# Two attentions whose value products alternate between output halves, with score tiles of 64 rows and one masked-maximum step

## The chip, the cores and the metric

The kernel runs on one core of a Trainium2 chip. The metric is the device time of one execution in microseconds (us); shorter is better. The engines are PE (matrix products: MATMUL, with its weight loads as a row of their own, PEld), DVE (VectorE), ACT (ScalarE), POOL (GpSimd) and SP, which issues loads. PE writes to PSUM only; a tile named `mm`, `bg` or `ax` lies there, a tile named `b` in SBUF.

## The reference, cut to what matters

Two transformer blocks run over 256 tokens of a stream x and 256 of a context. Most of the work is feed-forward and projection products. The change touches the two softmax attentions over 512 keys. In the first block (the "odd" mixer) there are 16 heads of 64 features; keys and values are shared by four heads each, a window mask covers the keys of x, and a learned `sink` takes part in the softmax:

```python
s_band = where(valid, einsum('bqhgd,bkhd->bhgqk', qj, kj), -inf)   # valid: |q - k| <= 128
s_ctx = einsum('bqhgd,bkhd->bhgqk', qj, kc)
p = softmax(concatenate([sink, s_ctx, s_band], -1), -1)
out = einsum('bhgqk,bkhd->bqhgd', p_ctx, vc) + einsum('bhgqk,bkhd->bqhgd', p_band, vj)
```

In the second block (latent attention, called MLA below) there are 16 heads with 96 features in a score and 64 in a value, without mask and sink:

```python
p = softmax(scale * (q_nope . k_nope + q_rope . k_rope), -1)
out = p @ v
```

## The kernel before, in words

Everything is float32. A product that needs precision in the large projections is made of three products of parts, hi·hi, hi·lo and lo·hi, each part exact in the format fp32r (`split`, L604 and L605, makes the parts: ACT the hi, DVE the lo). Products of plain float32 tiles, such as the values, are issued by the compiler as two MATMULs each.

Both attentions call `attention(units, pre, order)`. A unit is one head and 128 of the 256 queries against all 512 keys; each attention has 32 units, and `order` is "s0 e1 n1 t3 v4 f0": in step i the scores of unit i are emitted, exponential and normalisation of unit i-1, transposes of unit i-3, value products of unit i-4, and then filling work. Per unit:

- `st0`: `scores()` leaves [128 queries, 512 keys] in a PSUM tile of pool `mm` (5 tiles). DVE takes the negated maximum (L1427) and, in the odd mixer, the minimum of it and -sink (L1429).
- `st1`: ACT makes exp(score - max) with the row sum (L1436, followed by a read of the accumulator), and exp(sink - max) (L1439); DVE adds the two (L1440).
- `st2`: DVE takes the reciprocal (L1444) and scales the row (L1445).
- `st3`: PE transposes four 128x128 squares (L1451) into a PSUM tile `ax` (2 tiles), and ACT copies it to SBUF as PT (L1453).
- `st4`: `values(PT)`: four products of V[b], 64 columns wide, with 128 columns of PT each, summed in one half of a PSUM tile: partitions 0 to 63 for s = 0, 64 to 127 for s = 1 (`tile_position=(0, 64*s)`; L1578 in the odd mixer, L2213 in MLA). After eight units `split` takes the tile away.

In the odd mixer a score needs 64 rows only. The keys of two heads lie in one tile, features on partitions; before, `k_split` (L1508) makes for each key head s a pair of tiles in which the other 64 rows are zero, set by POOL. So each unit issues three products of 128 rows by 512 columns (L1567, L1569, L1570) and between them one bf16 product of the identity with the mask, 128 columns (L1568). In MLA a score is three products of 96 rows (L582 to L584).

Units that follow each other are s = 0 and s = 1 of the same head group and queries. The tile framework orders the instructions of each engine when the kernel is built, by what it expects to be ready; each engine then issues in that order. The weights of the projections come by DMA from the queue of SP, and ACT and DVE split them (L574, L575). The other column-tiled product of the kernel is the output of the state-space scan, `y` (L2349), whose inner loop alternates s = 0 and s = 1.

Of the kernel before, what the change touches and what calls it, by code (L numbers as in the profile page):

```python
# [48 lines left out]
F32 = mybir.dt.float32  # L49
# [7 lines left out]
P = 128  # L57
# [11 lines left out]
# ---------------------------------------------------------------- host layout  # L69
# [44 lines left out]
def _pack_tok(w):  # L114
    """Pieces of 4 blocks of rows by 512 columns, the column halves one after the other."""
# [181 lines left out]
# ---------------------------------------------------------------- the program  # L297
# [5 lines left out]
class Beat:  # L303
    """Emission order of work that waits on long chains: after(k, f) emits f once k more blocks of products are out."""
# [23 lines left out]
class Prog:  # L328
# [19 lines left out]
    def in_order(self):  # L348
        """Each compute engine issues what this block emits in the order of its emission."""
# [11 lines left out]
    def behind_now(self):  # L361
        """What this block emits is issued behind what has been emitted."""
# [9 lines left out]
    def behind(self):  # L372
        """What this block emits is issued behind the last block in order."""
# [7 lines left out]
    # ---- tiles  # L381
# [13 lines left out]
    def po(self):  # L395
        """Accumulators of attention outputs, alternating between two pools."""
# [23 lines left out]
    def consts(self):  # L420
# [7 lines left out]
        self.cstb = cp.tile([P, 3 * P], BF16, name="cstb")  # L428
# [20 lines left out]
    # ---- modulation vectors  # L449
# [5 lines left out]
    def mods(self, ci, w, bias, M, i0, cnt, post):  # L455
        """Steps that compute modulation vectors i0 .. i0+cnt-1 of M, one weight slab each."""
# [86 lines left out]
    def tick(self, n=1.0):  # L543
        """Emit background steps worth n."""
# [41 lines left out]
    def pair3(self, ps, W, X, first, last):  # L586
        """Both halves of one block of rows, the products that need the lo part of X behind the others."""
# [19 lines left out]
    # ---- rms statistics of one half (256 tokens), features on partitions  # L607
# [23 lines left out]
    def rstd2(self):  # L631
        """r1 = rms(h)^-1 and r12 = r1 * rms(h * fin * r1)^-1, as columns r12, r12, r1, r1.
# [1869 lines left out]
```

## Time and profile before

| | |
|---|---|
| median of 3 runs | 2310.92 us (2307.32 to 2318.86) |
| profiled execution, its span (the page tells its time by this) | 2305.9 us |
| instructions | 33864 |
| PE busy over the span | 2247.0 us, 97% |
| DVE, ACT, POOL busy over the span | 1564.9, 975.2, 166.7 us |
| odd attention, first score product to last value product | 1448.6 to 1532.5 us of the span |
| MLA attention, the same | about 1980 to 2081 us |

The page names PE first, and the chain of work that ended last is 76% PE. A matmul's end is modelled and overlaps the next one's start, so the cost of a matmul is read from one start to the next, not from its duration. On ACT and DVE too an instruction begins about 0.1 us before the one ahead is put down as ended, so the busy time of a stretch (in which overlaps count once) is less than the sum of the durations.

### The profile page before, as it was taken

Reading aid. Unit: us, or ns where it says so; the run is one execution under the profiler, and the core shown is the slowest. Engines: PE = TensorE matmul, PEld = TensorE weight load, DVE = VectorE, ACT = ScalarE, POOL = GpSimd, SP = SyncE. Lnnn points to the kernel's source line nnn. Section 1 sums busy time; section 2 is a strip of 40 time slices with the busy share of each in tenths; the row PEclk is TensorE's granted clock in tenths of the full one; section 3 lists DMA queues with packets and bytes.
Section 4 is the critical chain, followed back from the end, with each engine's and each line's share of the span. In section 5 each row is a group of like instructions: output and inputs, shape, how many; then the busy total and the mean of one; then the engine's idle time right before and its main releaser. Section 6 shows DMA issues by size and latency. Waiting matters only on the chain.

```text
span 2305.9 us, 33864 instructions
## 1 busy us (share of the span) xinstructions
PE 2247.0 (97%) x13706; PEld 1956.2 (85%) x13706; DVE 1564.9 (68%) x2447; ACT 975.2 (42%) x1651; POOL 166.7 (7%) x185
## 2 busy tenths in 40 slices
PE   7999999999899999999999999999999899999998
PEld 6888888888898888898878889789999788888997
DVE  5887774734897666468748647757556898666664
ACT  4222223544542222243222335656445566665553
POOL 0000000001300000000000002101000553000000
PEclk8999999999999999999999999999999999999999
DMA  7665552221145455325657623114554323213553
GB/s 266 218 232 182 185 204 83 92 101 74 56 160 187 155 192 183 146 92 201 242 173 285 231 92 115 57 56 169 184 183 160 133 88 122 85 60 126 184 175 120
DMA packets 58076, 348.54 MB, mean 151 GB/s; under 512 B 6464, under 2 KB 10048, under 8 KB 22848
## 3 DMA queue, kind: packets, MB, share of 16 engines
q1 hardware_dynamic: 56544, 344.22, 42.1%
q8 instruction: 108, 1.77, 0.3%
q0 software_dynamic: 512, 1.05, 0.2%
q10 hardware_dynamic: 864, 1.11, 0.2%
q14 instruction: 48, 0.39, 0.0%
HBM read 343.73 MB, written 1.05 MB: 150 GB/s over the span
## 4 chain that ended last, share of the span: by engine, by line
PE 76%; issue 13%; DVE 5%; POOL 3%; ACT 1%; DMA 1%; SPq 0%; POOLq 0%; DVEq 0%; ACTq 0%
PE mm L582 21%; PE mm L584 20%; PE mm L583 20%; PE mm L591 6%; PE ax L1451 1%; DVE wl L575 1%; POOL b L1727 1%; PE bg L531 1%; PE bg L1578 1%; PE bg L2213 1%; PE mm L1578 1%; PE mm L2213 1%; DMA b<-mod 1%; POOL b L1728 1%; DVE acc L616 0%
## 5 line engine op out<-in xcount | busy, mean ns | idle before, releaser
L582 PE MATMUL mm<-b,wh 128*128 128x512 f32 (+1 forms) x2764 | 958.5, 348 | 3.6 <-DVE c L1617 1.9
L584 PE MATMUL mm<-b,wl 128*128 128x512 f32 (+1 forms) x2764 | 947.7, 344 | 3.6 <-DVE wl L575 3.5
L583 PE MATMUL mm<-b,wh 128*128 128x512 f32 (+1 forms) x2764 | 949.5, 344 | 0.0
L575 DVE TENSOR_TENSOR wl<-wr,wh 128x1024 fp32r<-128x1024 f32 (+2 forms) x474 | 553.7, 1173 | 392.0 <-ACT wh L574 385.5
L574 ACT CAST wh<-wr 128x1024 fp32r<-128x1024 f32 (+2 forms) x474 | 473.7, 1006 | 575.8 <-PE mm L583 389.8
L582 PEld LDWEIGHTS mm<-b,wh 128*128 128x128 f32 x2764 | 527.0, 191 | 78.3 <-issue 8.5
L584 PEld LDWEIGHTS mm<-b,wl 128*128 128x128 f32 x2764 | 526.1, 191 | 65.7 <-DVE wl L575 5.0
L583 PEld LDWEIGHTS mm<-b,wh 128*128 128x128 f32 x2764 | 527.3, 191 | 61.0 <-issue 1.9
L522 DVE SCALAR_TENSOR_TENSOR ma<-mr,cs,ma 128x1024 f32<-128x1024 f32 x252 | 311.5, 1278 | 32.9 <-DMA mr<-ada 28.8
L591 PE MATMUL mm<-b,wh 128*128 128x256 f32 x1408 | 254.5, 283 | 0.0
L591 PEld LDWEIGHTS mm<-b,wh 128*128 128x128 f32 x1408 | 220.3, 192 | 0.2 <-ACT b L604 0.2
L591 PE MATMUL mm<-b,wl 128*128 128x256 f32 x704 | 184.4, 283 | 0.0
L591 PEld LDWEIGHTS mm<-b,wl 128*128 128x128 f32 x704 | 135.5, 192 | 0.0
L927 ACT ACTIVATE s<-mm 128x512 f32<-128x512 f32 x66 | 39.5, 599 | 222.2 <-PE mm L584 222.1
L582 PE MATMUL mm<-wh,b 128*128 128x512 f32 (+1 forms) x264 | 100.1, 380 | 1.9 <-ACT b L604 1.9
L583 PE MATMUL mm<-wl,b 128*128 128x512 f32 (+1 forms) x264 | 99.5, 377 | 0.0
L584 PE MATMUL mm<-wh,b 128*128 128x512 f32 (+1 forms) x264 | 99.3, 377 | 0.0
L629 POOL TENSOR_TENSOR rr<-rv,nhalf 128x2 f32<-128x2 f32 x15 | 15.6, 1043 | 991.6 <-DVE rv L628 991.6
L604 ACT CAST b<-s 128x512 fp32r<-128x512 f32 x70 | 43.2, 617 | 73.4 <-DVE s L928 64.9
L928 DVE TENSOR_TENSOR s<-s,mm 128x512 f32<-128x512 f32 x66 | 45.2, 684 | 40.3 <-PE mm L584 40.3
L1427 DVE TENSOR_REDUCE mx<-mm 128x1 f32<-128x512 f32 x64 | 43.8, 687 | 31.9 <-PE mm L1570 17.5
L983 DVE SCALAR_TENSOR_TENSOR h<-mm,M,h 128x256 f32<-128x256 f32 x144 | 59.6, 476 | 7.5 <-PE mm L584 7.5
(357 smaller groups left out, 2072.8 us busy)
## 6 DMA issues: line engine op xcount, KB each, us to landing
wr<-win SPq DMA_DIRECT2D x88, 1024.0 KB, 4.8
mr<-ada SPq DMA_DIRECT2D x56, 1024.0 KB, 4.9
wr<-wout SPq DMA_DIRECT2D x40, 768.0 KB, 4.4
mr<-mod SPq DMA_DIRECT2D x26, 1024.0 KB, 5.0
wr<-b_up SPq DMA_DIRECT2D x22, 1024.0 KB, 4.9
wr<-wout SPq DMA_DIRECT2D x14, 1024.0 KB, 4.8
wr<-b_xbc SPq DMA_DIRECT2D x11, 1024.0 KB, 4.9
wr<-b_down SPq DMA_DIRECT2D x10, 1024.0 KB, 4.9
```

Source lines behind the costliest of these rows:

```text
L522: nc.vector.scalar_tensor_tensor(hold["a"][s][:, c], raw[:, c], v, hold["a"][s][:, c], op0=ALU.mult, op1=ALU.add)
L574: nc.scalar.copy(hi, r)
L575: (nc.gpsimd if k0 // kk in pool else nc.vector).tensor_sub(lo, r, hi.bitcast(F32))
L582: nc.tensor.matmul(ps, lhsT=ah, rhs=bh, start=first, stop=False)
L583: nc.tensor.matmul(ps, lhsT=ah, rhs=bl, start=False, stop=False)
L584: nc.tensor.matmul(ps, lhsT=al, rhs=bh, start=False, stop=last)
L591: nc.tensor.matmul(ps[:, HS[q]], lhsT=l[:, P * q:P * q + P], rhs=r, start=first and q == 0 and l is wh and r is xh, stop=last and q == 1 a ...
L928: nc.vector.tensor_mul(s, s, pu)
L983: nc.vector.scalar_tensor_tensor(h[:, m, c], ps[:, c], M[:, ig, m, half:half + 1], h[:, m, c], op0=ALU.mult, op1=ALU.add)
L1427: nc.vector.tensor_reduce(mx, S[u], axis=AX.X, op=ALU.max, negate=True)
L1578: nc.tensor.matmul(po[64 * s:64 * s + 64, (g % 2) * 256 + qb * P:(g % 2) * 256 + qb * P + P], lhsT=V[b][:, kv * 64:kv * 64 + 64], rhs=PT[: ...
L2213: nc.tensor.matmul(po[64 * s:64 * s + 64, col:col + P], lhsT=V[pair // 4, tb][:, hd * 64:hd * 64 + 64], rhs=PT[:, tb * P:(tb + 1) * P], st ...
```

## The change

- **Values, both attentions.** `values` of s = 0 only keeps its PT; that of s = 1 issues all eight products, and in its inner loop the two heads alternate (z = 0, 1), so that neighbouring products write different halves of the PSUM tile. The sums are the same.
- **Scores, odd mixer.** `scores` of s = 0 issues the products of both heads at once, into two PSUM tiles: each product takes 64 rows of the query and key tile, at `tile_position=(64*z, 0)`. The zero-padded key tiles and POOL's eight clears of half a tile go; `KZ` holds one pair of tiles for two heads.
- **Mask, maximum and sink, odd mixer.** The mask product is gone. Two mask tiles are built once (POOL clears, DVE copies). One DVE step (L1428 after) reads the scores from PSUM and the mask from SBUF, writes -(score + mask) to SBUF, and gives min over the row and -sink; the kernel built issues it as two instructions, the second on a 128x1 tile. The exponential then reads SBUF with scale -1 and writes in place.
- The bf16 copy of the constants at the kernel's start is gone with the mask product. Comments were removed; line numbers move.

```diff
@@ attention: st0 and st1
-            S[u] = scores()
+            S[u], mask = scores()
             mx = mxs[u] = self.tmp([P, 1], "mx", 6)
-            nc.vector.tensor_reduce(mx, S[u], axis=AX.X, op=ALU.max, negate=True)
-            if sink is not None:
-                nc.vector.tensor_tensor(mx, mx, sink[1], op=ALU.min)
+            if mask is not None:
+                t = self.b2()
+                nc.vector.tensor_tensor_reduce(out=t, in0=S[u], in1=mask, scale=-1.0, scalar=sink[1], op0=ALU.add,
+                                               op1=ALU.min, accum_out=mx)
+                S[u] = t
+            else:
+                nc.vector.tensor_reduce(mx, S[u], axis=AX.X, op=ALU.max, negate=True)
...
+                pr = prs[u] = S.pop(u)
+                nc.scalar.activation(pr, pr, AF.Exp, scale=-1.0, bias=mx, accum_out=rs)
@@ odd: scores and values
-                nc.tensor.matmul(S, lhsT=qh[:, qc], rhs=kh, start=True, stop=False)
-                nc.tensor.matmul(S[:, mcol], lhsT=identb, rhs=mk, start=False, stop=False)
-                nc.tensor.matmul(S, lhsT=qh[:, qc], rhs=kl, start=False, stop=False)
-                nc.tensor.matmul(S, lhsT=ql[:, qc], rhs=kh, start=False, stop=True)
+                for i, (x, y) in enumerate(((qh, kh), (qh, kl), (ql, kh))):
+                    for z in range(2):
+                        r = slice(64 * z, 64 * z + 64)
+                        nc.tensor.matmul(S[z], lhsT=x[r, qc], rhs=y[r], start=i == 0, stop=i == 2,
+                                         tile_position=(64 * z, 0))
...
                 for b in range(4):
-                    nc.tensor.matmul(po[64 * s:64 * s + 64, (g % 2) * 256 + qb * P:(g % 2) * 256 + qb * P + P],
-                                     lhsT=V[b][:, kv * 64:kv * 64 + 64], rhs=PT[:, b * P:(b + 1) * P],
-                                     start=b == 0, stop=b == 3, tile_position=(0, 64 * s), skip_group_check=True)
+                    for z, t in enumerate((hold["PT"], PT)):
+                        v = (2 * a_ + z) * 64
+                        nc.tensor.matmul(po[64 * z:64 * z + 64, col:col + P], lhsT=V[b][:, v:v + 64],
+                                         rhs=t[:, b * P:(b + 1) * P], start=b == 0, stop=b == 3,
+                                         tile_position=(0, 64 * z), skip_group_check=True)
```

`values` in `mla` is changed in the same way. Outside the two attentions and the few instructions named, the order of instructions on every engine is as it was. Three places show what the order on PE becomes. A row of it is a line number, the operation, the tile written, the tiles read and the size of the output; "x4" means four in a row. L1451, L1578 and L2213 before are L1457, L1592 and L2231 after, and the score lines L1567 to L1570 are L1576.

First, PE in the middle of the odd attention, between two units before: transposes, four value products of one head, three score products with the mask product among them, transposes.

```order
L1451 MATMUL ax_12501<-cst,b_12439 128x128 x4
L1578 MATMUL bg_12318<-b_12479,b_11382 64x128
L1578 MATMUL bg_12318<-b_12479,b_11409 64x128
L1578 MATMUL bg_12318<-b_12479,b_11280 64x128
L1578 MATMUL bg_12318<-b_12479,b_11307 64x128
L1567 MATMUL mm_12516<-b_11569,b_11779 128x512
L1568 LDWEIGHTS cstb
L1568 MATMUL mm_12516<-cstb 128x128
L1569 MATMUL mm_12516<-b_11570,b_11779 128x512
L1570 MATMUL mm_12516<-b_11569,b_11780 128x512
L1451 MATMUL ax_12532<-cst,b_12466 128x128 x4
```

The same place after, from the last score product of a pair of heads on; `b_12472` is ACT's copy of `ax_12467`.

```order
L1576 MATMUL mm_12450<-b_11559,b_11767 128x512
L1457 MATMUL ax_12467<-cst,b_12371 128x128 x4
L1457 MATMUL ax_12484<-cst,b_12404 128x128 x4
L1592 MATMUL mm_12491<-b_12435,b_11380 64x128
L1592 MATMUL mm_12491<-b_12472,b_11380 64x128
L1592 MATMUL mm_12491<-b_12435,b_11407 64x128
L1592 MATMUL mm_12491<-b_12472,b_11407 64x128
L1592 MATMUL mm_12491<-b_12435,b_11278 64x128
L1592 MATMUL mm_12491<-b_12472,b_11278 64x128
L1592 MATMUL mm_12491<-b_12435,b_11305 64x128
L1592 MATMUL mm_12491<-b_12472,b_11305 64x128
```

The value products of two heads now stand together and alternate, the transposes of two units follow each other, and between the transposes that yield `b_12472` and the first product that reads it stand four transposes and one value product.

Second, PE near the start of the odd attention before: the score products of two units, s = 0 and s = 1, whose key tiles are padded.

```order
L1567 MATMUL mm_11762<-b_11489,b_11582 128x512
L1568 LDWEIGHTS cstb
L1568 MATMUL mm_11762<-cstb 128x128
L1569 MATMUL mm_11762<-b_11490,b_11582 128x512
L1570 MATMUL mm_11762<-b_11489,b_11583 128x512
L1567 MATMUL mm_11783<-b_11495,b_11582 128x512
L1568 LDWEIGHTS cstb
L1568 MATMUL mm_11783<-cstb 128x128
L1569 MATMUL mm_11783<-b_11496,b_11582 128x512
L1570 MATMUL mm_11783<-b_11495,b_11583 128x512
```

After, two pairs from the same stretch; `mm_11787` and `mm_11788` are the two tiles of one pair, `mm_11838` and `mm_11839` of the next.

```order
L1576 MATMUL mm_11787<-b_11487,b_11564 128x512
L1576 MATMUL mm_11788<-b_11487,b_11564 128x512
L1576 MATMUL mm_11787<-b_11488,b_11564 128x512
L1576 MATMUL mm_11788<-b_11488,b_11564 128x512
L1576 MATMUL mm_11787<-b_11487,b_11565 128x512
L1576 MATMUL mm_11788<-b_11487,b_11565 128x512
L1576 MATMUL mm_11838<-b_11487,b_11564 128x512
L1576 MATMUL mm_11838<-b_11488,b_11564 128x512
L1576 MATMUL mm_11838<-b_11487,b_11565 128x512
L1576 MATMUL mm_11839<-b_11487,b_11564 128x512
L1576 MATMUL mm_11839<-b_11488,b_11564 128x512
L1576 MATMUL mm_11839<-b_11487,b_11565 128x512
```

The first pair alternates between the two row halves as the source has it; in the second the three products of one half stand ahead of the three of the other.

Third, PE in MLA before: scores, transposes, the four value products of one unit.

```order
L582 MATMUL mm_18490<-b_17548,b_18090 128x512
L583 MATMUL mm_18490<-b_17549,b_18090 128x512
L584 MATMUL mm_18490<-b_17548,b_18090 128x512
L1451 MATMUL ax_18501<-cst,b_18417 128x128 x4
L2213 MATMUL bg_18508<-b_18455,b_18165 64x128
L2213 MATMUL bg_18508<-b_18455,b_18222 64x128
L2213 MATMUL bg_18508<-b_18455,b_18259 64x128
L2213 MATMUL bg_18508<-b_18455,b_18302 64x128
```

The same stretch after; L581 to L583 are products of a projection.

```order
L1457 MATMUL ax_18449<-cst,b_18366 128x128 x4
L2231 MATMUL bg_18456<-b_18375,b_18089 64x128
L581 MATMUL mm_18465<-b_17024,wh_18283 128x256
L582 MATMUL mm_18465<-b_17025,wh_18283 128x256
L583 MATMUL mm_18465<-b_17024,wl_18284 128x256
L581 MATMUL mm_18465<-b_17024,wh_18283 128x256
L582 MATMUL mm_18465<-b_17025,wh_18283 128x256
L583 MATMUL mm_18465<-b_17024,wl_18284 128x256
L2231 MATMUL bg_18456<-b_18430,b_18089 64x128
L2231 MATMUL bg_18456<-b_18375,b_18141 64x128
L2231 MATMUL bg_18456<-b_18430,b_18141 64x128
L2231 MATMUL bg_18456<-b_18375,b_18183 64x128
```

Here the first value product of the pair has been put ahead of other work, alone, and the other seven follow behind it.

## Rows read from the trace of the kernel before

**Rows 1.** The page: busy time, share of the span and instructions.

```profile
PE 2247.0 (97%) x13706; PEld 1956.2 (85%) x13706; DVE 1564.9 (68%) x2447; ACT 975.2 (42%) x1651; POOL 166.7 (7%) x185
```

**Rows 2.** Stretches of both attentions: length, busy PE, PEld, DVE, ACT, POOL; clock, DMA.

```profile
1448.60:1532.50 83.90, 82.29 (x528) 60.10 (x527) 56.27 (x185) 56.31 (x146) 4.66 (x3) 1.00 0.08 27
1980.00:2081.00 101.00, 101.00 (x641) 82.07 (x639) 67.80 (x144) 67.51 (x146) 8.37 (x15) 1.00 0.22 71
```

**Rows 3.** Waits, odd attention: who waited for whom, us in all, times, longest.

```profile
DVE mx L1427 <- PE mm L1570: 17.5, 21, 2.6
ACT b L1453 <- PE ax L1451: 17.0, 22, 1.3
```

**Rows 4.** Timeline of PE, one unit, odd: start, us to last end, count.

```profile
1472.66 0.60 PE L1451 MATMUL ax<-cst,b 128*128 128x128 f32 x4
1473.19 1.09 PE L1578 MATMUL bg<-b,b 128*64 128x128 f32 x8
1474.21 0.50 PE L1567 MATMUL mm<-b,b 128*128 128x512 f32 x1
...
1475.14 0.60 PE L1451 MATMUL ax<-cst,b 128*128 128x128 f32 x4
1475.66 0.32 PE L1578 MATMUL bg<-b,b 128*64 128x128 f32 x1
```

**Rows 5.** Timeline of PE, odd, half a block of value products.

```profile
1461.76 0.65 PE L1578 MATMUL bg<-b,b 128*64 128x128 f32 x4
1462.34 0.66 PE L1451 MATMUL ax<-cst,b 128*128 128x128 f32 x4
```

**Rows 6.** Timeline of PE, the state-space output, whose halves alternate.

```profile
1882.85 1.97 PE L2349 MATMUL mm<-b,b 128*64 128x128 f32 x32
1884.74 0.49 PE L728 MATMUL ax<-cst,rr 128*128 128x128 f32 x2
```

**Rows 7.** Timeline of PE, one unit of MLA.

```profile
1995.37 0.50 PE L582 MATMUL mm<-b,b 96*128 96x512 f32 x1
...
1995.94 0.39 PE L584 MATMUL mm<-b,b 96*128 96x512 f32 x1
1996.17 0.60 PE L1451 MATMUL ax<-cst,b 128*128 128x128 f32 x4
1996.70 1.09 PE L2213 MATMUL bg<-b,b 128*64 128x128 f32 x8
```

**Rows 8.** Groups on DVE, whole span: out<-in, form, count, busy us, mean ns.

```profile
L522 DVE SCALAR_TENSOR_TENSOR ma<-mr,cs,ma 128x1024 f32<-128x1024 f32 x252 | 311.5, 1278 | 32.9 <-DMA mr<-ada 28.8 <-DMA mr<-mod 3.8
...
L1427 DVE TENSOR_REDUCE mx<-mm 128x1 f32<-128x512 f32 x64 | 43.8, 687 | 31.9 <-PE mm L1570 17.5 <-PE mm L584 14.2
...
L1429 DVE TENSOR_TENSOR mx<-mx,nsink 128x1 f32<-128x1 f32 x32 | 4.8, 153 | 0.0
...
L1140 DVE SCALAR_TENSOR_TENSOR s<-mm,prm,b 128x512 f32<-128x512 f32 x4 | 3.0, 748 | 4.6 <-PE mm L1136 4.6
...
L1242 DVE TENSOR_TENSOR_SCAN b<-b,b 32x512 f32<-32x512 f32 x1 | 1.2, 1202 | 0.0
```

**Rows 9.** Groups on ACT, odd attention.

```profile
L1453 ACT COPY b<-ax 128x512 f32<-128x512 f32 x32 | 18.7, 585 | 17.1 <-PE ax L1451 17.0
...
L604 ACT CAST b<-b 128x512 fp32r<-128x512 f32 x2 | 1.2, 618 | 2.8 <-POOL b L1532 2.8
L604 ACT CAST b<-mm 128x512 fp32r<-128x512 f32 x2 | 1.2, 586 | 1.6 <-PE mm L1578 1.6
```

**Rows 10.** Timeline of PE, odd: the first score product, the first transposes.

```profile
1448.62 0.80 PE L1567 MATMUL mm<-b,b 128*128 128x512 f32 x1
...
1457.94 0.66 PE L1451 MATMUL ax<-cst,b 128*128 128x128 f32 x4 [0.66 <-DVE b L1445]
```

**Rows 11.** Timeline of all engines, odd: one copy of transposed rows.

```profile
1473.30 0.59 ACT L1453 COPY b<-ax 128x512 f32<-128x512 f32 x1 [0.63 <-PE ax L1451]
```

**Rows 12.** A group on PE, odd attention.

```profile
L1567 PE MATMUL mm<-b,b 128*128 128x512 f32 x32 | 15.4, 482 | 0.9 <-ACT b L1436 0.8
```

More of the change, by code (lines that the diff above doesn't have):

```diff
@@ L848, in start @@
         load_mod(0)
-        nc.vector.tensor_copy(self.cstb, self.cst)
         self.silu_c(0, "cv")
@@ L1433, in st1 @@
             mx = mxs.pop(u)
-            pr = prs[u] = self.b2()
             rs = rss[u] = self.tmp([P, 1], "rs", 6)
-            nc.scalar.activation(pr, S.pop(u), AF.Exp, bias=mx, accum_out=rs)
-            if sink is not None:
+            if sink is None:
+                pr = prs[u] = self.b2()
+                nc.scalar.activation(pr, S.pop(u), AF.Exp, bias=mx, accum_out=rs)
+            else:
+                pr = prs[u] = S.pop(u)
+                nc.scalar.activation(pr, pr, AF.Exp, scale=-1.0, bias=mx, accum_out=rs)
                 es = self.tmp([P, 1], "es", 6)
@@ L1507, in k_split @@
             nc.vector.tensor_add(kx[b][:, 0:256], t1[:, 0:256], t2[:, 0:256])
-            for s in range(2):
-                hi, lo = self.b2(F32R), self.b2(F32R)
-                oth = slice(64 - 64 * s, 128 - 64 * s)
-                me = slice(64 * s, 64 * s + 64)
-                nc.gpsimd.memset(hi[oth].bitcast(F32), 0.0)
-                nc.gpsimd.memset(lo[oth].bitcast(F32), 0.0)
-                self.split(kx[b][me], hi[me], lo[me])
-                KZ.append((hi, lo))
+            KZ.append((self.b2(F32R), self.b2(F32R)))
+            self.split(kx[b], *KZ[b])
         XX = self.xhalf(X, 0)
@@ L1554, in odd @@
         nc.vector.tensor_scalar_mul(nsink, sink, -1.0)
-        identb = self.cstb[:, 0:P]
+        masks = []
+        for qb in range(2):
+            mask = self.b2()
+            nc.gpsimd.memset(mask, 0.0)
+            nc.vector.tensor_copy(mask[:, (1 - qb) * P:(2 - qb) * P], self.maskn[1 - qb])
+            masks.append(mask)
         AT, units, hold = [], [], {}
@@ L1562, in scores @@
             def scores():
[L1563 removed]
+                if s == 1:
+                    return hold["S"], masks[qb]
+                S = [self.mm(), self.mm()]
                 qh, ql = Q[j]
[L1565 to L1568 removed]
@@ L2203, in scores @@
                 self.mac3(S, qh[r96, qc], ql[r96, qc], kh[r96], kl[r96], True, True)
-                return S
+                return S, None
             def values(PT):
-                if (pair % 2, qb, s) == (0, 0, 0):
+                if s == 0:
+                    hold["PT"] = PT
+                    return
+                if (pair % 2, qb) == (0, 0):
                     hold["po"] = self.po()
                 po = hold["po"]
-                hd = (2 * pair + s) % 8
                 col = (pair % 2) * 256 + qb * P
                 for tb in range(4):
-                    nc.tensor.matmul(po[64 * s:64 * s + 64, col:col + P], lhsT=V[pair // 4, tb][:, hd * 64:hd * 64 + 64],
-                                     rhs=PT[:, tb * P:(tb + 1) * P], start=tb == 0, stop=tb == 3,
-                                     tile_position=(0, 64 * s), skip_group_check=True)
-                if (pair % 2, qb, s) == (1, 1, 1):
+                    for z, t in enumerate((hold["PT"], PT)):
+                        hd = (2 * pair + z) % 8
+                        nc.tensor.matmul(po[64 * z:64 * z + 64, col:col + P],
+                                         lhsT=V[pair // 4, tb][:, hd * 64:hd * 64 + 64], rhs=t[:, tb * P:(tb + 1) * P],
+                                         start=tb == 0, stop=tb == 3, tile_position=(0, 64 * z), skip_group_check=True)
+                if (pair % 2, qb) == (1, 1):
                     hi, lo = self.b2(F32R), self.b2(F32R)
```

16 lines of the change are left out of this document (9 added, 7 removed).

## The prediction

> **What bounds the kernel now.** I read the page first: PE is busy for 97% of the span, DVE for 68%, ACT for 42% [rows 1]. An average over stages does not say what one stage is worth, so next the windows of the two attentions. In the odd one PE is busy for 82.3 of 83.9 us, DVE and ACT for 56.3 each; in MLA PE for all of 101, DVE 67.8, ACT 67.5; the granted clock is 1.00, the level of 2.4 GHz, in both [rows 2]. The waits of the odd attention point the same way: DVE waits 17.5 us for scores, ACT 17.0 us for transposes [rows 3]. PE sets the pace of both, with 28 us of slack on the others in the odd attention and 33 us in MLA. So the change is worth what it takes off PE until another engine, or the way around all three, becomes late.
>
> A unit in the odd attention is a cycle of 2.47 us on PE: values from 1473.19, scores and mask from 1474.21, transposes from 1475.14, the next values at 1475.66, so 1.02, 0.93 and 0.52 us [rows 4]. 32 of them make 79 us.
>
> **The change part by part.** *Values.* Eight MATMULs take 1.02 us and four take 0.58 [rows 4, 5], so one costs 0.11, and a block of eight 0.14 beyond its eight. In the state-space output, of the same form but with halves that alternate, 32 take 1.89 [rows 6]: less 0.14, 0.055 each. Neighbours on different halves overlap, and two cost what one does. Each attention has 32 x 8 = 256, or 28.2 us. After, 128 slots of 0.11 are 14.1. The built order does not keep all pairs whole: in ten of the odd attention's sixteen the first product stands alone, ahead of other work, as in the third place of the order shown. It leaves 27 blocks in the odd attention and 25 in MLA, and each ends or begins with one that has no partner: 27 x 0.11 = 3.0 and 25 x 0.11 = 2.8. Saved: 28.2 - 14.1 - 3.0 = 11.1 us (odd) and 11.3 (MLA).
>
> *Mask product.* The score block with it takes 0.93 [rows 4], the block of MLA without it 0.80 [rows 7], so it costs 0.13; 32 are 4.2 us saved.
>
> *Scores by 64 rows.* A 512-column score product costs 0.23 from start to start [rows 7], three 0.69. The change still issues six for two heads. No row shows two row halves at work together, so the bounds are no gain, and 0.69 per pair of heads. The built order alternates in ten of sixteen pairs only; in the other six the three products of one half come first, for which I count nothing. I take the upper end, since the nearest row, the column halves [rows 6], overlaps fully, less a fifth because three of the ten pairs are cut by another block: 10 x 0.69 x 0.8 = 5.5 us saved, bounds 0 and 6.9.
>
> The Trainium skill, "TensorE: Matmul & The Clock Gate", Part 3 (Measured speedup vs the span model), gives four row tiles of 32 rows 3.07 times the speed of one. An estimate from that page for two tiles, at the same share of the ideal, is 1.5 times, and the term would be 4.6 instead of 5.5. No row here shows row tiles.
>
> *Mode changes.* The 0.14 beyond a block's eight, and the 0.08 that the four transposes ahead of it take beyond 4 x 0.11 [rows 4], are the way into another tiling of the array and out of it: 0.22 for two changes, 0.11 each. Scores now have a tiling of their own. Counted in the built order, changes in the odd attention go from 67 to 82, +15 x 0.11 = 1.7 us. In MLA, blocks of values go from 31 to 25, two changes each: 1.3 saved. A change to row tiles is not in the trace; I take the same price.
>
> PE in the odd attention: 82.3 - 11.1 - 4.2 - 5.5 + 1.7 = 63.2 us of work.
>
> *The DVE step.* Maximum and minimum cost 0.687 + 0.153 [rows 8]. The new step reads PSUM and SBUF, adds, and keeps a minimum. Its nearest row is a step of two tensors and a scalar at 0.748; its ends are the plain maximum at 0.687 and the scan, which also carries a value along the row, at 1.20 [rows 8]. I take 0.748 and, for the second instruction on a 128x1 tile, 0.153. That is +0.06 x 32 = 2.0, and half a us for two mask copies: DVE 56.3 + 2.5 = 58.8, under PE's 63.2, hidden. *The exponential* now reads SBUF. Where ACT casts the same size from SBUF and from PSUM it takes 0.618 and 0.586 [rows 9]: +0.03 x 32 = 1 us, ACT 57.3, hidden. POOL's clears, two of four casts and subtractions in `k_split`, and the copy of constants at the start lie under PE's projections; I count them as nothing, at most 1 us of gain. SP's loads keep their order.
>
> *What PE waits for instead.* With PE at 63 and the others at 57 to 59, a wait costs something. First, the start: between the first score at 1448.6 and the first transposes at 1457.9 PE has only scores to do, because the first row must pass DVE, ACT and DVE [rows 10]. These 9.3 us do not shrink with the scores, and the scores in them get about 3 us shorter: 3 us not gained. Second, the copy of transposed rows. The last of four transposes starts at 1472.66 + 0.33, ACT's copy begins at 1473.30 and takes 0.59 [rows 4, 11], so values may read it 0.9 after that start. Before, another unit's transposes and scores lay between; now four transposes (0.44), a mode change (0.11) and one value product (0.22), about 0.8, and the products queued behind it, with the next scores, wait as well. If ACT is free, this is nothing. If an exponential is ahead, it is up to 0.7. ACT would be busy four fifths of the time: I take 0.25 a pair, 16 x 0.25 = 4 us, bounds 0 and 11. In MLA the scores of a unit (0.80) lie between too; I take 1.5, bounds 0 and 8.
>
> **Sum.** Odd: -11.1 - 4.2 - 5.5 + 1.7 + 3 + 4 = -12.1. MLA: -11.3 - 1.3 + 1.5 = -11.1. Together -23.2 us of the profiled execution's span of 2305.9, so 2282.7. The median lies 5.0 above that span, and what lies around the span does not change: 2310.9 - 23.2 = 2287.7.
>
> **The rivals.**
> 1. *Row halves don't overlap.* Then 5.5 is missing: -17.7, 2293. For it: no row of it. Against it: column halves do [rows 6].
> 2. *The DVE step runs at the scan's rate.* DVE gets 32 x 0.45 = 14.5 more, 73.3, and becomes the bound; with 6 at the ends where it can't work the odd attention takes 79 instead of 83.9: total -16, 2295. Against it: a step with two f32 operands and a scalar runs 1024 columns in 1.278 [rows 8], the full rate. The Trainium skill, "Vector Engine (DVE) Microarchitecture Reference", Points that are easy to get wrong, says that this family with two non-bf16 sources in SBUF runs at half throughput; the trace disagrees (1.278 us for 1024 columns), and here one source is in PSUM.
> 3. *The copy's wait costs its upper bound in both attentions.* 11 instead of 4 and 8 instead of 1.5: -23.2 + 13.5 = -9.7, 2301. For it: ACT and DVE close to PE, all issuing in a fixed order. Against it: ACT's copies wait for PE today [rows 3].
> 4. *The order undoes it.* Should lone products and cut pairs leave values unpaired, about the mask's 4.2 remains: 2306. Against it: 7 or 8 of each block alternate in the order.
> 5. *Slower.* If the array has to run empty between two row halves, each score product costs its full duration, 0.48 [rows 12], and a mode change, 0.11, or 0.59 instead of 0.23 or less. PE then has 63.2 - 16.6 + 96 x 0.59 = 103 us in the odd attention, with 7 of waits 110, 26 more than now; less MLA's 11.1, +15: 2326. It decides for slower by over 0.5% from 0.55 each. Against it: a mode change costs 0.11 today, not a duration.
>
> **How the numbers follow.** 0.5% is 11.6 us, about what a measurement of this kernel can tell from no change. Chances: forecast 0.53, no overlap of rows 0.13, scan rate 0.08, copy wait 0.15, order 0.05, slower 0.06. The forecast has its own range from 2279 (scores at 6.9, no copy wait, 1 at the start) to 2294. Case 3 lies about the line of 2299.4, so half of it counts as faster: 0.53 + 0.13 + 0.08 + 0.07 = 0.81; same 0.08 + 0.05 = 0.13; slower 0.06. The range takes in cases 1 and 2 and most of 3: 2277 to 2302.
>
> **What would show it.** In the profile after, 16 value MATMULs in an unbroken pair should take about 1.0 us from start to start (0.055 each), in both attentions; six alternating score products about 0.7 to 0.9, against 1.4 if rows don't overlap and 3.5 in rival 5. The DVE step should take 0.75 and its second part 0.15; 1.2 would be rival 2. PE's busy time in the odd attention should be about 63 to 66 in a stretch of about 72, with new idle time ahead of value products that ends with ACT's copy; in MLA the stretch should be about 90. The rest of the span should be as before to 1 us. I am wrong if the row-tiled products cost more than 0.23 each, if PE's idle time exceeds 12 us in the odd attention, or if MLA gains under 8.

## The result and the profile after

The changed kernel takes 2286.22 us (median of 4 runs, 2283.40 to 2286.85) against 2311.39 for the kernel before beside it: a ratio of 0.9881, 95% interval 0.9863 to 0.9900. The prediction was 2287.7 in a range of 2277 to 2302. The profiled run's span fell from 2305.9 to 2284.5, by 21.4, where 23.2 was forecast. The medians are 25.2 apart: the profiled span of the kernel before lies 5.5 under its median, that of the changed kernel 1.7. The number is right; as the rows below show, it is so by luck, since two errors of about the same size cancelled.

To compare kernels whose earlier stages end a microsecond sooner or later, two stretches are used from here on, both cut at rows of the timeline of PE. *Odd* runs from the first score product to the first product of the output projection: 1448.62 to 1531.96 before, 83.34 us, which is the window of [rows 2] without its last half microsecond. *MLA* runs from the first transposes to the first product of the next projection: 1984.47 to 2080.13 before, 95.66 us. Odd fell to 72.55 (-10.8; forecast -12.1), MLA to 82.74 (-12.9; forecast -11.1). The time outside the two is 2.3 us longer after, where the prediction had it as before to 1 us. PE runs at 1.2 GHz for 41 us of it in both traces, so the clock does not account for the 2.3, and their cause is open. The three together give the 21.4. Each stretch also holds some products of the next projection that were issued early, 4 (before) to 15 (e11) of 0.12 us in odd beside what the table marks, 25 to 28 of 0.23 us in MLA; so two rows of the table are to be compared to about 1 us.

The windows of both attentions in the changed kernel, columns as in [rows 2]:

```profile
1450.10:1522.65 72.55, 70.16 (x499) 46.81 (x498) 56.29 (x187) 54.61 (x145) 3.79 (x3) 0.88 0.09 31
1972.00:2061.00 89.00, 89.00 (x647) 71.53 (x647) 66.84 (x144) 66.66 (x147) 8.41 (x15) 1.00 0.25 81
```

MLA is about as forecast: its window is 89 us against "about 90", with PE busy for all of it. The odd row has what the prediction did not foresee: a granted clock of 0.88 instead of 1.00. The same stretch in windows of 4 us shows where:

```profile
1448.00:1452.00 4.00, 4.00 (x22) 2.14 (x20) 3.00 (x5) 2.40 (x3) 1.14 (x1) 1.00 0.19 29
1452.00:1456.00 4.00, 2.11 (x13) 1.15 (x12) 2.55 (x5) 2.08 (x3) 2.52 (x2) 1.00 0.61 250
1456.00:1460.00 4.00, 3.64 (x10) 2.22 (x10) 3.90 (x12) 3.23 (x10) 1.27 (x1) 0.57 0.00 0
1460.00:1464.00 4.00, 3.86 (x15) 2.17 (x15) 3.68 (x14) 3.01 (x9) 0.00 (x0) 0.50 0.01 2
1464.00:1468.00 4.00, 4.00 (x21) 2.77 (x17) 1.46 (x5) 0.66 (x2) 0.00 (x0) 0.50 0.00 0
1468.00:1472.00 4.00, 4.00 (x13) 2.21 (x11) 1.82 (x7) 2.26 (x6) 0.00 (x0) 0.50 0.00 0
1472.00:1476.00 4.00, 4.00 (x31) 2.98 (x29) 1.95 (x9) 2.69 (x7) 0.00 (x0) 0.80 0.01 4
```

PE has little to do after the first scores (2.11 of 4 us), and then, from 1456.5 to 1473.6, 17.1 us long, it is granted 0.50, the level of 1.2 GHz. PE looks full there, but its products are half as fast, and DVE and ACT stand idle behind it (busy for 1.46 and 0.66 of 4 us in the fifth row). The kernel before, in the second and third of these windows, has more to do, and its clock stays at 1.00:

```profile
1452.00:1456.00 4.00, 3.17 (x14) 1.59 (x13) 3.13 (x7) 3.51 (x7) 2.04 (x3) 1.00 0.38 150
1456.00:1460.00 4.00, 3.22 (x18) 1.94 (x17) 4.00 (x16) 3.35 (x13) 0.68 (x1) 1.00 0.00 0
```

The timeline of PE shows the thin place and the price of one block:

```profile
1450.12 0.96 PE L1576 MATMUL mm<-b,b 64*128 64x512 f32 x6
1451.01 1.12 PE L1396 MATMUL ax<-b,perm 128*128 128x512 f32 x2
1452.07 2.04 PE L1576 MATMUL mm<-b,b 64*128 64x512 f32 x12
1456.36 2.92 PE L1576 MATMUL mm<-b,b 64*128 64x512 f32 x6 [2.25 <-DVE mx L1428]
1459.20 2.34 PE L1457 MATMUL ax<-cst,b 128*128 128x128 f32 x8
...
1463.67 1.97 PE L1592 MATMUL bg<-b,b 128*64 128x128 f32 x14
...
1476.55 1.09 PE L1592 MATMUL bg<-b,b 128*64 128x128 f32 x14
```

L1576 are the 64-row scores, L1592 the value products. The scores of three pairs of heads are soon done, and the fourth pair has to wait 2.25 us for PSUM tiles that DVE still reads. The same 14 value products take 1.97 us in the slow stretch and 1.09 behind it.

What holds the start is not the softmax of the first row alone. Its masked maximum is done at 1453.1, but the first exponential begins 2.7 us later: ahead of it in the order of ACT stand the cast of a projection's part, which waits for POOL's rotation (L1532), and a table load of 1.28 us.

```profile
1452.35 0.74 DVE L1428 CUSTOM_DVE_ANT_0 b<-mm,b,nsink 128x512 f32<-128x512 f32 x1
1452.57 1.29 POOL L1532 TENSOR_TENSOR b<-b,b 128x512 f32<-128x512 f32 x1 [3.43 <-DVE b L1405]
1453.89 0.62 ACT L603 CAST b<-b 128x512 fp32r<-128x512 f32 x1 [3.10 <-PE mm L1576]
1454.53 1.28 ACT L1443 ACT_TABLE_LOAD   x1
1455.82 0.72 ACT L1443 ACTIVATE b<-b,mx 128x512 f32<-128x512 f32 x1
```

The wait of the cast is put down to PE, which had long been done; POOL's step ends at 1453.86, and in e4 the same 3.10 us are put down to `POOL b L1532`. The kernel before has both too. No run here takes these two out of the way.

The steps on DVE and ACT in the odd attention (groups: shapes, count, busy us, mean ns) answer to [rows 8, 9]:

```profile
L1428 DVE CUSTOM_DVE_ANT_0 b<-mm,b,nsink 128x512 f32<-128x512 f32 x32 | 23.8, 744 | 0.4 <-PE mm L1576 0.4
...
L1428 DVE DVE_READ_ACCUMULATOR2_ANT mx<- 128x1 f32 x32 | 2.7, 85 | 0.0
...
L1443 ACT ACTIVATE b<-b,mx 128x512 f32<-128x512 f32 x32 | 23.1, 722 | 0.7 <-DVE mx L1428 0.6
L1459 ACT COPY b<-ax 128x512 f32<-128x512 f32 x32 | 18.3, 582 | 10.7 <-PE ax L1457 10.6
```

### The profile page after: what moved, and what is told of

It is laid out like the page before. It is cut to its first block, busy times and chain, and to the rows that moved or that the text cites. A ratio compares the mean times of both kernels' runs of the same rounds, so it can differ in the third digit from the quotient of the medians.

```text
span 2284.5 us, 33769 instructions
## 1 busy us (share of the span) xinstructions
PE 2226.4 (97%) x13674; PEld 1934.4 (85%) x13674; DVE 1562.5 (68%) x2446; ACT 971.9 (43%) x1649; POOL 164.1 (7%) x179
## 4 chain that ended last, share of the span: by engine, by line
PE 76%; issue 13%; DVE 5%; POOL 2%; ACT 2%; DMA 1%; SPq 0%; POOLq 0%; DVEq 0%; ACTq 0%
PE mm L581 21%; PE mm L583 21%; PE mm L582 21%; PE mm L590 6%; PE ax L1457 2%; PE mm L1576 1%; DVE wl L574 1%; PE bg L530 1%; POOL b L1741 1%; POOL b L1742 1%; PE bg L1592 1%; DVE acc L615 0%; POOL rr L628 0%; DMA wr<-wout 0%; PE mm L1592 0%
## 5 line engine op out<-in xcount | busy, mean ns | idle before, releaser
L581 PE MATMUL mm<-b,wh 128*128 128x512 f32 (+1 forms) x2764 | 958.5, 348 | 3.3 <-DVE c L1631 1.9
L583 PE MATMUL mm<-b,wl 128*128 128x512 f32 (+1 forms) x2764 | 948.0, 344 | 3.7 <-DVE wl L574 3.7
L581 PEld LDWEIGHTS mm<-b,wh 128*128 128x128 f32 x2764 | 527.2, 191 | 78.0 <-issue 8.1
L583 PEld LDWEIGHTS mm<-b,wl 128*128 128x128 f32 x2764 | 526.5, 191 | 65.9 <-DVE wl L574 5.6
L581 PE MATMUL mm<-wh,b 128*128 128x512 f32 (+1 forms) x264 | 101.0, 383 | 1.9 <-ACT b L603 1.9
L583 PE MATMUL mm<-wh,b 128*128 128x512 f32 (+1 forms) x264 | 99.8, 379 | 0.0
L762 ACT ACTIVATE b<-v,M 128x256 fp32r<-128x256 f32 x88 | 40.4, 501 | 47.6 <-DVE v L758 47.6
```

The source lines that it names most:

```text
L581: nc.tensor.matmul(ps, lhsT=ah, rhs=bh, start=first, stop=False)
L583: nc.tensor.matmul(ps, lhsT=al, rhs=bh, start=False, stop=last)
L762: nc.scalar.activation(xh, v, AF.Identity, bias=sh)
```

## The experiments

Theory A: in both attentions the gain is overlap on PE, and in the odd one the shorter scores leave PE too little to do before the first transposes, after which its clock falls and takes back 6 to 8 us. Theory B: the odd attention is held by waits around PE, ACT's copies above all. Theory C: the fall has nothing to do with the scores. All results, with the two stretches and the clock of the first:

| kernel | median us | ratio to before (95%) | odd us | clock | MLA us |
|---|---|---|---|---|---|
| before | 2311.39 | | 83.34 | 1.00 | 95.66 |
| after | 2286.22 | 0.9881 (0.9863 to 0.9900) | 72.55 | 0.88 | 82.74 |
| e1 values only | 2283.50 | 0.9876 (0.9859 to 0.9892) | 71.73 | 1.00 | 82.75 |
| e2 scores only | 2305.50 | 0.9979 (0.9969 to 0.9989) | 78.41 | 0.96 | 95.67 |
| e3 values, mask step | 2283.08 | 0.9873 (0.9858 to 0.9888) | 68.92 | 1.00 | 82.75 |
| e4 after + filler | 2280.47 | 0.9865 (0.9850 to 0.9880) | 66.20 | 1.00 | 82.74 |
| e5 e1, thin start | 2286.05 | 0.9884 (0.9862 to 0.9905) | 71.52 | 0.98 | 82.74 |
| e6 projection at start | 2287.13 | 0.9885 (0.9863 to 0.9907) | 74.37* | 0.95 | 82.74 |
| e7 e6 + order | 2277.88 | 0.9857 (0.9838 to 0.9876) | 72.71* | 0.98 | 79.35 |
| e8 e4, halves in turn | 2285.84 | 0.9890 (0.9875 to 0.9905) | 71.83 | 1.00 | 82.74 |
| e9 after again | 2285.57 | 0.9884 (0.9868 to 0.9900) | 73.54 | 0.88 | 82.74 |
| e10 projection later + order | 2278.67 | 0.9845 (0.9827 to 0.9864) | 71.29* | 1.00 | 79.30 |
| e11 e4 + order | 2275.71 | 0.9838 (0.9816 to 0.9859) | 65.59 | 1.00 | 79.33 |

\* holds one query projection, 5.7 us of PE, that stands ahead of the stretch in the others.

**e1: the value products alone.** The kernel before with this in `odd`, and the same in MLA:

```diff
-                for b in range(4):
-                    nc.tensor.matmul(po[64 * s:64 * s + 64, ...], ..., rhs=PT[:, b * P:(b + 1) * P], ...)
+                for b in range(4):
+                    for z, t in enumerate((hold["PT"], PT)):
+                        nc.tensor.matmul(po[64 * z:64 * z + 64, ...], ..., rhs=t[:, b * P:(b + 1) * P], ...)
```

> The kernel before, with the value products alternating in both attentions and nothing else. Theory A (the fall of the granted clock at the start of the odd attention comes from the shorter scores, which leave PE too little to do before the first transposes): the start is as in the kernel before, the clock stays 1.00, the odd attention takes 11 us less than 83.9 (about 73), MLA 12 less than 101 (about 89); together -23, about 2288, no slower than the whole change. Theory B (the waits around PE, on ACT's copies, eat the gain in the odd attention): odd gains 5 or less, MLA 12, together about -16, 2295. Theory C (the clock's fall has nothing to do with the scores): the 1.2 GHz stretch stands here too, odd gains about 4, 2295.

Odd 71.73 (-11.6), MLA 82.75 (-12.9), the clock 1.00: theory A's 11 and 12 less to 1 us, and no sign of B, whose 5 or less is far off. One of the three edits is as fast as all of them (2283.5 against 2286.2). The window of the odd stretch:

```profile
1448.87:1520.60 71.73, 70.11 (x528) 48.71 (x527) 56.05 (x185) 54.76 (x145) 4.66 (x3) 1.00 0.09 31
```

**e2: the scores and the mask step alone.** The changed kernel with the value products of before:

> The whole change without the alternating value products (in both attentions a block of values is one head's, as before): 64-row score tiles and the DVE step alone. Theory A: the scores and the mask take 8 us off the odd attention at full clock, but the start is that of the changed kernel, so the clock falls to 0.50 after the first scores and about 7.5 us are lost: odd within 2 us of 83.9, MLA as before (101), the whole -1 to -3, about 2309. Theory C: the clock stays at 1.00: odd about 76, the whole -8, about 2303.

The clock falls here too, at 1455.4, but for 6.8 us instead of 17. Odd is 78.41 (-4.9), the whole 0.21% faster: the edits to the scores bring something, about twice what A allowed for, which fits the shorter fall. So the fall goes with these edits and not with the values; its length is not given by them alone. Windows of 4 us from 1452, columns as above:

```profile
1452.00:1456.00 4.00, 1.76 (x11) 0.95 (x8) 2.55 (x6) 2.71 (x5) 2.45 (x2) 0.93 0.48 190
1456.00:1460.00 4.00, 3.87 (x11) 2.30 (x12) 3.90 (x11) 2.88 (x10) 1.27 (x1) 0.50 0.00 0
1460.00:1464.00 4.00, 4.00 (x27) 3.09 (x27) 3.60 (x15) 3.37 (x10) 0.00 (x0) 0.72 0.01 2
```

**e3: values and mask step, but scores of 128 rows.** The changed kernel with the zero-padded keys of before:

```diff
-                S = [self.mm(), self.mm()]
-                ...  six products on 64 rows
+                S = self.mm()
+                self.mac3(S, qh[:, qc], ql[:, qc], kh, kl, True, True)
```

> The whole change without the 64-row tiles: scores are three full products a head against keys padded with zeros, as before, the mask product is gone and the DVE step does mask, maximum and sink; values alternate. Without a fall of the clock odd gains 11 (values) + 4 (mask product) = 15 and takes about 69, MLA 89: together -27, about 2284, better than the whole change. With a fall (the start has 0.7 instead of 0.93 us of work per head): odd about 76, together -19, 2292. Theory A expects the start to lie between the two kernels, so the clock is the open question here; theory B expects no more than -17.

Odd 68.92 at clock 1.00, where about 69 was expected without a fall: 2.8 less than e1, which is the mask product and the step on DVE, and 3.6 less than the whole change. In the odd stretch the 64-row tiles, as they stand, cost the change more than they bring; the medians (2283.1 and 2286.2) have intervals that overlap.

**e4: something to do for PE.** The changed kernel with 20 products whose result nobody reads, at the thin place:

```diff
+        def filler(n):
+            t = self.gp.tile([P, 512], F32, tag="bg", name=self.name("bg"))
+            qh, kh = Q[0][0], KZ[0][0]
+            for i in range(n):
+                nc.tensor.matmul(t, lhsT=qh[:, 0:P], rhs=kh, start=i == 0, stop=i == n - 1)
+
+        late[3].append(lambda: filler(20))
```

> The whole change plus 20 score products whose result nobody reads, behind the scores of the first two pairs of heads, where PE would be idle until the first transposes: it adds 20 x 0.23 = 4.6 us of work to PE. Theory A: the granted clock stays 1.00 through the odd attention and the stretch goes from 73.4 to about 66: together with the rest 7 less than the changed kernel, about 2279. Theory B (the odd attention is held by waits, the clock is a by-product): the same as the changed kernel or up to 4.6 slower, 2286 to 2291.

With 4.8 us more work the odd attention is 6.35 us shorter than in the changed kernel, 66.20, as theory A said to 0.2 us, and the whole 2280.5. Its start, and the window of the stretch:

```profile
1451.78 0.96 PE L1583 MATMUL mm<-b,b 64*128 64x512 f32 x6
1452.67 1.13 PE L1396 MATMUL ax<-b,perm 128*128 128x512 f32 x2
1453.73 0.97 PE L1583 MATMUL mm<-b,b 64*128 64x512 f32 x6
1454.62 4.83 PE L1556 MATMUL bg<-b,b 128*128 128x512 f32 x20
1460.91 0.63 PE L1457 MATMUL ax<-cst,b 128*128 128x128 f32 x4 [1.45 <-DVE rs L1446]
```

```profile
1451.78:1517.98 66.20, 64.14 (x519) 44.52 (x518) 56.16 (x187) 54.28 (x145) 3.83 (x3) 1.00 0.10 34
```

The first transposes come 9.1 us behind the first score, as in the changed kernel: the filler lies in time that PE could not use. The mean granted clock of all runs, profiled or not, agrees: 0.985 to 0.990 in the eight of the changed kernel (after and e9), 0.990 to 0.994 in the twelve of e1, e3 and e4, and 17.1 us at 0.50 take 0.004 off the mean. The odd attention's -10.8 is the way from before to e1 (-11.6, values), to e3 (-2.8, mask), to e4 (-2.7, 64-row scores) and to the changed kernel (+6.35). Not all of this last step is the clock. With the filler the framework orders PE anew, and the traces of e4 have 24 blocks of scores where the changed kernel has 26, and 25 blocks of values instead of 27. At the prices found below (0.36 us for a lone value product, 0.2 to 0.43 for a cut in the scores) that is an estimated 1 us, which leaves 5 to 6 us to the clock.

**e5: a thin start and nothing else.** e1 with the second and third score product of the first six units left out:

```diff
+                thin = a_ == 0 and 2 * g + qb < 3
+                if thin:
+                    return S
```

> e1_values_only, with two of the three score products left out for the first six units only (their scores are the high part alone): the start of the odd attention gets 12 x 0.23 = 2.8 us less work on PE, and nothing else of the change is in it. In e1 the stretch from the first score to the first product of the output projection was 71.7 us at a granted clock of 1.00. Theory A: the clock now falls to 0.50 behind the first scores, for 7 to 17 us, and although work was left out the stretch is 74 to 78: 2286 to 2290. Theory C (the 64-row form or the DVE step, not the thin start, goes with the fall): clock 1.00, stretch 70 to 72, 2281 to 2284.

The clock falls, at 1457.6, in a kernel with neither 64-row tiles nor the DVE step, which speaks against theory C, though in one trace. But it falls for 3.4 us only, and the stretch was expected at 74 to 78 and is 71.5, no longer than e1's. From the first transposes on it takes 63.69 us against e1's 62.40.

**e6 and e7: useful work in place of the filler.** e6 moves the last query projection behind the first pair's scores; e7 also issues the later head's values first:

```diff
-        q_proj(3)
-        late = {0: [lambda: q_mul(2)], 1: [lambda: q_split(2)], 2: [lambda: q_mul(3)], 3: [lambda: q_split(3)]}
+        late = {0: [lambda: q_mul(2)], 1: [lambda: q_proj(3), lambda: q_split(2)], 4: [lambda: q_mul(3)],
+                5: [lambda: q_split(3)]}
...
-                    for z, t in enumerate((hold["PT"], PT)):
+                    for z, t in ((1, PT), (0, hold["PT"])):
```

> The whole change with the last of the four query projections (48 products, 5.7 us of PE) moved behind the first pair's scores, so that useful work stands where PE was idle and the clock fell. Theory A: the clock stays 1.00 (worth the 6.3 us that e4 got back) and the idle time before the first transposes (4.6 us filled by e4's products at no loss) is filled with work that the program has to do anyway: 6.3 + 4 = 10 less than the changed kernel, about 2275. Theory B (the first transposes, not PE's work, set the end of the start, and moving the projection only delays its own rotation and split into the attention): 6 or less, 2280. Slower would mean that the weight split of that projection, now beside the first softmax steps on ACT and DVE, delays them.

> e6 with the value products of each pair issued with the later head first, in both attentions, so that no value product can stand alone ahead of other work. Prediction's term: a lone product costs its 0.11 without a partner, and a block of two takes 0.36 instead of 0.11 because of its own mode changes; with 9 to 10 such places in each attention 0.25 x 10 = 2.5 us less in each, 5 together against e6. Rival: the lone product stood where PE would have waited for ACT's copy anyway, so nothing is gained or the wait grows: within 2 us of e6.

e6 fails: 2287.1. PE stands idle at other places instead, behind the moved projection, and the clock falls there, at 1455.5, for 6.8 us in the profiled run. That run took 2278.2, with a mean granted clock of 0.994; the three others, 2286.8 to 2288.4, were 9 us longer with 0.987 to 0.991. So they lost more to the clock, but no trace of them shows where. The two rows of PE around the fall:

```profile
1453.56 0.63 PE L1457 MATMUL ax<-cst,b 128*128 128x128 f32 x4 [1.12 <-DVE b L1451]
1454.93 1.51 PE L1396 MATMUL ax<-b,perm 128*128 128x512 f32 x2 [0.74 <-ACT b L1525]
```

In e7 the clock falls there too, at 1454.5 and for 3.4 us. e7 shows the price of lone products cleanly in MLA, at clock 1.00 in both: 82.74 to 79.35, -3.4. There nine blocks of two and nine of 14 took 0.36 and 1.02 us in the changed kernel; now blocks of 16 take 1.02 and the nine times 0.36 are gone.

**e8: the halves in turn.** e4 with the two loops around the score products exchanged:

```diff
-                for i, (x, y) in enumerate(((qh, kh), (qh, kl), (ql, kh))):
-                    for z in range(2):
+                for z in range(2):
+                    for i, (x, y) in enumerate(((qh, kh), (qh, kl), (ql, kh))):
```

> e4_filler_at_start with the three score products of one 64-row half emitted before the three of the other, so that neighbours share a half: if two halves overlap only as neighbours (0.89 us for six alternating products with a mode change, against 6 x 0.23 + 0.11 = 1.5), about 0.5 us per pair of heads in the odd attention, 16 x 0.5 = 8 at most: stretch 66.2 to 70 or 74, 2284 to 2288. If the overlap is worth nothing here (waits take its place): stretch 66 to 67, 2280.

The stretch is 5.6 us longer, within what was expected, for another reason. Six products in turn still take 0.90:

```profile
1449.47 0.97 PE L1583 MATMUL mm<-b,b 64*128 64x512 f32 x6
1450.37 1.12 PE L1396 MATMUL ax<-b,perm 128*128 128x512 f32 x2
...
1481.39 0.96 PE L1583 MATMUL mm<-b,b 64*128 64x512 f32 x3
1482.28 0.66 PE L1457 MATMUL ax<-cst,b 128*128 128x128 f32 x4
...
1490.37 1.09 PE L1457 MATMUL ax<-cst,b 128*128 128x128 f32 x8
1491.39 0.49 PE L1583 MATMUL mm<-b,b 64*128 64x512 f32 x2
```

The records of those six begin in pairs, 10 ns apart: the second half's first product starts with the first half's first, though three stand ahead of it. So the halves need not be neighbours, only in one unbroken block, whose time is that of its fuller half, 0.23 for each product, and 0.2 for the modes: 0.43, 0.66, 0.89 for one, two, three. What e8 loses is in the cuts. In turn, a cut block of three holds one half (0.89), a cut block of five again three of one half (0.89), and the order has 30 score blocks instead of 24 and three whole ones instead of eight: 22.0 us against 17.3 in e4, counted from the start of each block to the next instruction's. That is 4.7 of the 5.6 us.

**e9: the changed kernel again.**

> The changed kernel unaltered, timed beside the next one on the same chip. Theory A (its start makes the clock fall, not one unlucky execution): a stretch at 0.50 begins again within 2 us of the place 6 us behind the first score, and the odd attention takes 70 to 74 us, 2283 to 2287. If the fall of the first profile was an accident: clock 1.00 there, about 66 us, 2279.

The clock falls at 1458.1, 8.6 us behind the first score (6.4 in the first profile), again for 17.1 us; odd is 73.54. No accident.

**e10 and e11: a version that beats both?** e10 puts the projection where e4 has its filler, its weights loaded and split where they were, and has e7's order. e11 is e4 with e7's order.

```diff
+        W3 = self.wload(a["o_q"][3], KD, 256)
+        late = {0: [lambda: q_mul(2)], 1: [lambda: q_split(2)], 3: [lambda: q_proj(3, W3)], 6: [lambda: q_mul(3)],
+                8: [lambda: q_split(3)]}
```

> The changed kernel with the later head's value products first (e7) and the last query projection where e4 had its filler, behind the scores of two pairs of heads, its weights still loaded and split where they were before. e4's filler took 4.8 us there and left 1.5 idle, and cost nothing; the projection takes 5.7. Theory A: the clock stays 1.00 through the start as in e4 (odd 66.2, now with the projection in it), the 5.7 us are missing ahead of the attention, and the later-head order gives 3.4 in MLA (82.74 to 79.35 us in e7) and about 2 in the odd attention: against e4 5.7 - 1 + 5 = 10 less, about 2271. If the projection's rotation and split, now inside the attention on ACT, DVE and POOL, delay the softmax steps: 2274 to 2280. If the clock falls all the same, as in e6: 2277 to 2283.

> e4_filler_at_start with the later head's value products first, as in e7, so that the order is measured in the odd attention at a granted clock of 1.00 with nothing else moved. If a lone product costs its own mode changes (a block of two takes 0.36 us, and e4 has eight of them in the odd attention): the odd stretch goes from 66.2 to about 64, MLA from 82.74 to 79.35 as in e7, together 5 to 6 less than e4, 2275. If in the odd attention the order only moves the wait for ACT's copy: 66, MLA alone gains, 2277.

e10 keeps the clock at 1.00 through the stretch and needs 71.29 us with the projection in it, where e4's 66.20 and 5.7 outside would be 71.9. So hardly anything of the projection is hidden, and nothing against e11, which has the same order (65.59 + 5.7 = 71.3): the first transposes come 11.75 us behind the first score, 9.1 in e4. The rows of the other engines show why:

```profile
1446.43 0.99 POOL L1559 MEMSET b<- 128x512 f32 x2
...
1449.62 0.21 DVE L1560 COPY b<-cst 128x128 f32<-128x128 f32 x1
1449.75 0.74 DVE L1428 CUSTOM_DVE_ANT_0 b<-mm,b,nsink 128x512 f32<-128x512 f32 x1
1449.84 1.29 POOL L1532 TENSOR_TENSOR b<-b,b 128x512 f32<-128x512 f32 x1 [0.83 <-DVE b L1560]
...
1451.17 0.62 ACT L603 CAST b<-b 128x512 fp32r<-128x512 f32 x1 [4.03 <-POOL b L1532]
```

The projection had covered the making of the masks. POOL clears them (L1559) behind its rotations, DVE copies into them behind that, and so the first DVE step begins 6.3 us behind the first score instead of 2.2 (e4). Then ACT waits 4.03 us for POOL ahead of the first exponential. At 2278.7 it is no better than e7 and lies where the expectation put it for a delayed softmax. One run took 2270.8, with a mean granted clock of 0.995 against 0.987 to 0.990 in the others. e11 is the fastest of all, 2275.7, 0.5% under the changed kernel, though its 20 products compute nothing. The order gives it 3.4 in MLA and only 0.6 in the odd attention, though all value blocks there take 16.5 us instead of 21.0. The second expectation, that PE waits for the copy instead, is not what the rows show: the copy (L1459) is 0.2 us of PE's waits. PE's idle time does grow, from 2.1 to 3.8 us, but ahead of transposes, and the scores are cut into 27 blocks instead of 24 and take 19.9 instead of 17.3 us, some of that waiting.

PE's waits in e11's odd stretch (who waited for whom, us in all, times, longest), and the window of that stretch:

```profile
PE ax L1457 <- DVE rs L1446: 2.4, 3, 1.4
PE ax L1457 <- DVE b L1451: 0.6, 1, 0.6
PE ax L1457 <- ACT b L1443: 0.6, 1, 0.6
PE mm L1599 <- ACT b L1459: 0.2, 1, 0.2
```

```profile
1450.89:1516.48 65.59, 61.77 (x522) 42.96 (x522) 55.93 (x187) 54.18 (x145) 3.83 (x3) 1.00 0.10 34
```

## Why the prediction came out right, step by step

- **Values: right.** Forecast -11.1 and -11.3. e1 gives -11.6 in the odd attention. In MLA all value blocks took 32.1 us before and 19.6 after, -12.5, which is the forecast's -11.3 with its -1.3 of mode changes. Sixteen products in an unbroken block take what eight took [rows 4]: 1.02. The lone products were put down at 0.11 for each of 25 blocks, 2.8 us; in fact nine cut places cost 0.36 each, 3.3 us with their modes, and an unbroken block costs nothing more. In the odd attention taking them away brought only 0.6.
- **Mask: too high.** Forecast -4.2, e3 against e1 -2.8. From the first transposes on e3 takes 59.12 us against 62.40, -3.3; up to them it takes 9.81 against 9.33, so the mask products of the start bring nothing.
- **64-row scores: mis-sized, on the good side.** I let only ten of sixteen pairs overlap and took a fifth off. e8 shows that order inside a block does not matter, so nearly all did. Scores and mask took 32 x 0.93 = 29.8 before [rows 4] and 17.3 in e4: -12.5 at full clock, where the forecast has -4.2 - 5.5 + 1.7 = -8.0. That is work. In the stretch, mask and 64-row scores together brought 5.5 (e1 to e4), where the forecast with its 3 us of start has 5.0: what was saved beyond the forecast went to the start and to waits. A block of six is 0.2 + 3 x 0.23, so two half tiles run 2.0 times as fast as one. The estimate of 1.5 times from the Trainium skill, "TensorE: Matmul & The Clock Gate", Part 3, was too low for two tiles; the trace decides. The transposes give 1.6 us of it back, 16.5 to 18.1, since four cost 0.585 ahead of a row-tiled block.
- **DVE and ACT: hidden, as said.** The new step took 0.744 (forecast 0.748) and its second part 0.085 (0.153); DVE is busy for 56.3 us, not 58.8. The exponential took 0.722, up 0.035 as forecast.
- **The start: right, and not followed to its end.** The first transposes come 9.1 us behind the first score, 9.3 before [rows 10]. I counted 3 us of idle time there as "not gained" and stopped. I read the chain as DVE, ACT and DVE for one row, and did not see POOL's rotation and the table load ahead of the first exponential.
- **The clock: the step that failed.** I read 1.00 in [rows 2] and carried it over to the changed kernel. The idle time that I had just put down is followed by 17.1 us at 1.2 GHz, which cost 5 to 6 of the 6.35 us that e4 got back. No term, no rival and no line of "what would show it" had it.
- **The copy wait: too high.** Forecast 4 and 1.5. In e4, blocks of 16 that took 1.32 instead of 1.02 are the waits that can be seen, five of them and 1.5 us in all; in MLA every block of 16 took 1.02.

At full clock the odd attention would have come down by 16 to 17 us (17.1 in e4, with its better order), not 12.1, above all because the 4 us put down for the copy were not there; the changed kernel gave 6.35 of e4's 17.1 back, most of it to the clock, and MLA was better by 1.8. Of the rivals, the first and the fifth fall with the 0.2 + 3 x 0.23, the second with 0.744, the third with the 1.5 us of e4. The fourth, an order that undoes it, is a small part of the truth: 3.4 us in MLA.

## What to carry to other kernels

When an edit takes work off an engine, look for the place where that engine waits for a chain that does not get shorter, and ask what its clock may do there: a term of idle time may be followed by a longer stretch at half speed. Price each edit in a kernel of its own: here one of three cost more than it brought as it stood, and 20 products that compute nothing bought back 6 us. An edit also changes the order that the framework builds around it, so compare the blocks before calling a difference its price. Products on the two row halves overlapped within one unbroken block (e8), so there the block has to be kept whole, not the alternation.

## What the runs showed of the hardware that was not expected

- The granted clock fell from 1.00 to 0.50 behind a stretch in which PE was busy for 1.4 to 2.1 of 4 us (after, e2, e5, e6, e7, e9) and stayed there for 3.4 to 17.1 us, although PE was busy for nearly all of the time at half speed. What sets the length is open, and so is what exactly makes it fall. In e3 PE was busy for 1.97 of the 4 us from 1456, in e10 for 1.45 of the 4 us from 1452, behind 5.7 us of dense projection, and the clock stayed at 1.00 in both, so that a thin stretch alone does not decide it. The row of e3, and two of e10:

```profile
1456.00:1460.00 4.00, 1.97 (x7) 1.04 (x8) 3.90 (x12) 3.33 (x9) 1.27 (x1) 1.00 0.00 0
1448.00:1452.00 4.00, 4.00 (x36) 4.00 (x35) 2.68 (x6) 0.81 (x2) 2.31 (x2) 1.00 0.00 0
1452.00:1456.00 4.00, 1.45 (x12) 1.11 (x12) 3.56 (x12) 3.99 (x11) 0.00 (x0) 1.00 0.00 0
```

- A 64-row product started together with one of the other half that stood three places ahead of it in the queue (10 ns apart, e8).
- A lone 64-row product takes 0.43 us, nearly twice the 0.23 of a full one in a row of its like; cutting a block into two costs 0.2 to 0.43 us: a block of six at 0.89 becomes one of two and one of four (0.43 and 0.66) or one of one and one of five (0.43 and 0.89).
- Reading out the DVE accumulator took 85 ns, less than the 153 of the step on a 128x1 tile that it replaced.
